# Strided attention: four groups per store in the place of their Q blocks, dense turned weights, values 512 columns wide

## The chip, the cores and the metric

The kernel runs on one core of one Trainium2 chip. The metric is the device time of one execution in microseconds (us), the median of several runs. A profile is taken of one execution; its span runs from the first to the last instruction, and the execution's own time is a little longer than the span.

A core has five instruction queues that matter here, each in order: PE (matrix products; PEld is its weight loading), DVE, ACT and POOL (elementwise work on 128 partitions), and SP, which here only issues DMA transfers. Semaphores hold a queue's next instruction until another queue or a transfer is done. All transfers of this kernel go through SP's one DMA queue, spread over 16 DMA engines.

## The reference

Batch 8 and 12 heads make 96 heads, each with 1024 queries of 64 numbers (float32). Every query attends to the same 16 keys of its head, those at positions 0, 64, 128 and so on:

```python
q = Q[:, :, i:i + 1, :]
k = K[:, :, attend_positions, :]       # 16 keys
v = V[:, :, attend_positions, :]
scores  = einsum('bhqd,bhkd->bhqk', q, k) * scale
weights = exp(scores - max(scores))
weights = weights / (sum(weights) + 1e-10)
result  = einsum('bhqk,bhkd->bhqd', weights, v)
```

Q is 25.2 MB and so is the result. Of K and V only 0.4 MB each is needed. Arithmetic is small beside the 51 MB that have to be moved.

## The kernel before

**Tiling.** The 96 heads are cut into 24 groups of four heads (`HG = 4`, `NG = 24`). One group is 1 MiB of Q, 8 KB in each of 128 partitions, and 1 MiB of result.

**The way of one group g**, with the engine of each step:

- `load(g)` (SP): 1 MiB of Q into one of 11 blocks `qn` (`QBUFS = 11`).
- `cast(g)` (POOL, L307; for groups 0 to 2 shared with ACT, L302 and L304): to bf16 in `qb`.
- `transpose(g)` (DVE, L319): `qb` in 32x32 blocks of 4-byte words to `qt`.
- `scores(g)` (PE, L327): 16 products of 64 columns with the keys `k_t` into `sc`.
- `largest(g)` (DVE, L341 and L344): row maximum, and subtraction into the single buffer `low`.
- `raise_(g)` (ACT, L349): exponential into `ex`.
- `sums(g)` (DVE, L354 and L357): sum and reciprocal `rec`.
- `weights(g)` (POOL, L364): `ex * rec` to bf16 `wt`.
- `turn(g)` (PE, L371): four transposes of `wt` into `tp`.
- `spread(g)` (ACT, L383): two instructions copy `tp` to `wb`, each scaled by one column of the 0/1 mask `sel`, so that `wb` holds eight tiles of 128x128, half of each zero.
- `outputs(g, n)` (PE, L391), n = 0 and 1: four products of 256 columns each with the values `v_all`, into one half of the four-bank tile `o`.
- `evict(g, n)` (ACT, L411): that half of `o` to the block `out_sb` of the group. There are 8 such blocks (`OBUFS = 8`).
- `store(g, n)` (SP): single groups for the first 14 (`SINGLE = 14`) and for group 22, pairs between; the last group goes out by itself at the end. One row of result written in memory is 4 KB (16 queries of a head).

**The order of the work** is written out by hand. One turn i of the loop records the steps of several groups, newest first; the digit is how many groups a step lags behind (`cast-1` is group i + 1, `evA4` is group i - 4):

```python
ORDER = "transpose0 cast-1 values2 turn3 spread3 sums2 outA4 largest1 evA4 outB4 evB4 scores0 weights2 raise_1 queue4".split()
```

Each engine takes its own steps in that order. On POOL, therefore, `cast(i + 1)` stands ahead of `weights(i - 2)`; on DVE `transpose(i)`, `values`, `sums(i - 2)`, `largest(i - 1)`; on ACT `spread(i - 3)`, two evictions of group i - 4, `raise_(i - 1)`. `queue(i - 4)` puts a group's store and then the next loads on SP, so a load stands behind a store that waits for its evictions.

**Keys and values.** K and V are loaded once. `keys` (ACT, L278) places the keys in `k_t`. `values` (POOL, L291) copies the values from `v_raw` into `v_all`, which POOL had cleared (L264): 16 copies of 32 partitions in the turns 2 to 6, behind the casts.

**Waits.** `Program` records every step with what it reads and writes and turns that into semaphore waits; PE runs in a hardware loop and waits on counters (`gate`) instead. A step that carries a gate signals nothing else: who waits for `evict(g, 1)`, as a store does, waits for the next ACT step behind it, `raise_`.

Of the kernel before, what the change touches and what calls it, by code (L numbers as in the profile page):

```python
# [168 lines left out]
def kernel(  # L169
# [8 lines left out]
    nc = tc.nc  # L178
# [12 lines left out]
    QBUFS = 11  # L191
    OBUFS = 8
    RUN = 2
    SINGLE = 14
# [5 lines left out]
    qn = [sb.tile([P, 32 * D], FP32, name=f"qn{i}") for i in range(QBUFS)]  # L200
    out_all = [sb.tile([P, RUN, 2, 16, D], FP32, name=f"out_sb{i}") for i in range(OBUFS // RUN)]
    out_sb = [out_all[i // RUN][:, i % RUN] for i in range(OBUFS)]
    late = out_all[-1].rearrange("p n b x d -> p (n b x d)")
    k_raw = late[:, 0 : NC * D].rearrange("p (n d) -> p n d", d=D)
    k_half = late[:, NC * D : 2 * NC * D].bitcast(BF16).rearrange("p (a n d) -> p a n d", a=2, d=D)
    k_bf, k_r = [k_half[:, i] for i in range(2)]
# [6 lines left out]
    v_all = sb.tile([P, NG + 4, 4, D], BF16, name="v_all")  # L213
# [26 lines left out]
    def load_rows(name, tile_, src, lane):  # L240
        op("SP", lambda: nc.sync.dma_start(tile_, _ap_with(src, kv_src)),
           writes=[name], lane=lane)

    load_rows("k_raw", k_raw, K, f"out{OBUFS - 2}")
    load(0)
    load_rows("v_raw", v_raw, V, f"out{OBUFS - 1}")
    for g in range(1, QBUFS):
        load(g)
# [10 lines left out]
       writes=[f"wb{i}{a}" for i in range(2) for a in range(2)])  # L259
# [4 lines left out]
    op("POOL", lambda: nc.gpsimd.memset(v_all, 0.0),  # L264
       writes=[f"v{c}{a}{b}{m}" for c in range(2) for a in range(2) for b in range(2) for m in range(2)] + ["none"])
# [19 lines left out]
    parts = (slice(0, 2), slice(2, NC))  # L285
# [3 lines left out]
    def values(c, a, b, m):  # L289
        src, dst, part = 32 * (2 * c + b), 32 * (2 * a + b), parts[m]  # L290
        op("POOL", lambda: nc.gpsimd.tensor_copy(  # L291
            out=v_all[dst : dst + 32, 3 + c + 2 * part.start : 3 + c + 2 * part.stop - 1 : 2, 2 * a + b],
            in_=v_raw[src : src + 32, part],
        ), reads=["v_raw"] + apart, writes=[f"v{c}{a}{b}{m}"])
        apart[:] = [f"v{c}{a}{b}{m}"]
# [3 lines left out]
    def cast(g, shared):  # L299
        q, b = qn[g % QBUFS], qb[g % 2]  # L300
        if shared:
            op("ACT", lambda: nc.scalar.copy(b[:, half:], q[:, half:]),  # L302
               reads=[f"qn{g % QBUFS}1"], writes=[f"qb{g % 2}1"])
            op("POOL", lambda: nc.gpsimd.tensor_copy(out=b[:, 0:half], in_=q[:, 0:half]),  # L304
               reads=[f"qn{g % QBUFS}0"], writes=[f"qb{g % 2}0"])
        else:
            op("POOL", lambda: nc.gpsimd.tensor_copy(out=b, in_=q),  # L307
               reads=[f"qn{g % QBUFS}{h}" for h in range(2)] + apart,
               writes=[f"qb{g % 2}{h}" for h in range(2)])
            apart[:] = [f"qb{g % 2}0"]  # L310

    def transpose(g):
        k_in = {0: "0", 1: "1"}.get(g)
        words = qt[g % 2].bitcast(I32)
        if g >= NG:
            op("DVE", lambda: nc.vector.memset(qt[g % 2][:, 0:2], 0.0), reads=["low"], writes=[f"qt{g % 2}"],
               gate="turned")
            return
        op("DVE", lambda: nc.vector.transpose(  # L319
            _ap_with(words, [words.ap[0], [1, 2], [D, 16], [2, 32]]), qb[g % 2].bitcast(I32),  # L320
        ), reads=[f"qb{g % 2}0", f"qb{g % 2}1"] + [f"k_t{k_in}{h}" for h in range(4) if k_in],
           writes=[f"qt{g % 2}"], gate="turned")
# [37 lines left out]
    def weights(g):  # L360
        if g >= NG:
            op("POOL", lambda: nc.gpsimd.memset(wt[g % 2][:, 0:1, 0:2], 0.0), writes=[f"wt{g % 2}"], gate="weighted")
            return
        op("POOL", lambda: nc.gpsimd.tensor_tensor(  # L364
            out=wt[g % 2], in0=ex[g % 2],
            in1=rec[g % 2].unsqueeze(2).to_broadcast([P, 32, NK]), op=ALU.mult,
        ), reads=[f"ex{g % 2}", f"rec{g % 2}"] + [k for k in apart if k[0] == "v"], writes=[f"wt{g % 2}"], gate="weighted")

    def turn_products(g):
        for c in range(4):  # L370
            r = nc.tensor.transpose(  # L371
                tp_ps[g % 2][:, 2 * c : 2 * c + 2].rearrange("p a b -> p (a b)"),
                wt[g % 2][:, 8 * c : 8 * c + 8].rearrange("p t k -> p (t k)"), identity,
            )
        return r
# [5 lines left out]
    def spread(g):  # L381
        for a in range(2):
            op("ACT", lambda a=a: nc.scalar.activation(  # L383
                out=wb[g % 2][:, :, 64 * a : 64 * a + 64], in_=tp_ps[g % 2],
                func=AF.Copy, scale=sel[:, a : a + 1],
            ), reads=[f"tp{g % 2}", "sel"], writes=[f"wb{g % 2}{a}"])

    def output_products(g, k, n):
        for c in range(2 * n, 2 * n + 2):
            for u in range(2):  # L390
                r = nc.tensor.matmul(  # L391
                    _ap_with(
                        o_ps, [o_ps.ap[0], [128, 2], [256, 2], [1, D]],
                        extra_offset=512 * c + D * u,
                    ),
                    lhsT=wb[g % 2][:, 2 * c + u],
                    rhs=v_all[:, k].rearrange("p s d -> p (s d)"), start=True, stop=True,
                )
        return r

    def outputs(g, n):
        op("PE", None, reads=[f"wb{g % 2}0", f"wb{g % 2}1"] + [
               f"v{g % 2}{a}{b}{int(g >= 4)}" if 0 <= g < NG else "none" for a in range(2) for b in range(2)
           ], writes=[f"o{n}"], gates=[(f"free{n}", g + 1)] if g >= 0 else [], looped=True)

    def evict(g, n):
        to = out_sb[g % OBUFS].rearrange("p b (c x) d -> p c b (x d)", c=4)
        half = slice(2 * n, 2 * n + 2)
        plain = g >= NG - 1 - 2 * n
        ready = [f"wb{(g + 1) % 2}0", f"wb{(g + 1) % 2}1"] * (n == 0)  # L410
        op("ACT", lambda: nc.scalar.copy(  # L411
            to[:, half], o_ps[:, half].rearrange("p c (b x) -> p c b x", b=2)
        ), reads=[f"o{n}"] + ready, writes=[f"out{g % OBUFS}.{n}"] + ["k_raw", "k_bf", "k_r"] * (g == OBUFS - RUN and not n),
           after=[stored[g - OBUFS]] if g >= OBUFS and not n else [],
           gate=None if plain else f"free{n}", last=g == NG - 1 and n == 1)

        if plain:
            free([f"out{g % OBUFS}.{n}"], n)
# [12 lines left out]
    def store(g, n):  # L431
        both = range(g, g + n)
        sent = op("SP", lambda: send(g, n), lane=f"out{g % OBUFS}",
                  reads=[f"out{i % OBUFS}.{n}" for i in both for n in range(2)])
        stored.update((i, sent) for i in both)
# [20 lines left out]
    cast(2, True)  # L456
    sums(0)
# [5 lines left out]
    quadrants = [[(c, a, b, m) for c in range(2) for a in range(2) for b in range(2)] for m in range(2)]  # L463
    VALUES = {0: quadrants[0]}
    VALUES.update((i + 1, quadrants[1][2 * i : 2 * i + 2]) for i in range(4))

    DEPTH = 4
    turns = (NG + 4) // TURN
    ahead = 1

    def queue(g):
        for n in range(g + QBUFS + ahead if g else QBUFS, g + QBUFS + ahead + 1):
            if n < NG:
                load(n)
        if g < SINGLE or g == NG - 2:
            store(g, 1)
        elif g % RUN == RUN - 1 and g < NG - 1:
            store(g - RUN + 1, RUN)

    def at(i, stage, lag):  # L480
# [3 lines left out]
        if stage == "transpose" and 0 <= g < NG + 4:  # L484
# [3 lines left out]
        elif stage == "weights" and 0 <= g < NG + 2:  # L488
# [7 lines left out]
        elif stage in ("evA", "evB") and g == -1:  # L496
            n = int(stage == "evB")
            free(["wb00", "wb01"], n)
# [42 lines left out]
    end = send(NG - 1, 1)  # L541
# [34 lines left out]
```

## Time and profile before

| | |
|---|---|
| median of 3 runs | 129.38 us (129.22 to 129.51) |
| the profiled execution's own time | 128.91 us |
| its span | 126.7 us |
| busy PE / DVE / ACT / POOL | 67.0 / 86.4 / 96.8 / 81.8 us |
| DMA: moved, share of 16 engines' span that packets took | 51.16 MB, 96.5% |

The page of the profile has the busy time of each engine, the span in 40 slices, the DMA queues, and groups of instructions by line. A row of groups gives the line, engine, operation, output and input tile, count, busy time and the mean of one in ns, and the idle time of the engine ahead of them with what ended it. A row of the timeline gives start and length in us, engine, line, operation, count, and in brackets the idle time ahead of it. A row of windows gives for each engine its busy time and count in a stretch, then the granted PE clock, the share of the DMA engines' time and GB/s.

### The profile page before, as it was taken

The page shows a single profiled execution, that of the slowest core. Times are in us where ns is not written, and L with a number is a line of the kernel's source. Part 1 is how long each engine was busy: PE and PEld are TensorE (multiplying, and loading weights), DVE is VectorE, ACT ScalarE, POOL GpSimd, SP SyncE. Part 2 cuts the span into 40 slices and gives each one's busy share as a digit, 9 for nine tenths or more (in the row PEclk, how much of TensorE's full clock was granted, in tenths as well). Part 3 has the DMA queues.
Part 4 walks back from the last instruction along what each step waited for, and adds up shares of the span by engine and source line. Part 5 has one row for each costly group of instructions (what it writes and reads, how often), then busy time and mean ns, then how long its engine had stood idle before and what let it go on. Part 6 is the DMA issues. An engine that isn't in the chain of part 4 may idle for free. (4 is left out here: it accounts for less than half of the span.)

```text
span 126.7 us, 2269 instructions
## 1 busy us (share of the span) xinstructions
PE 67.0 (53%) x784; PEld 48.7 (38%) x784; DVE 86.4 (68%) x129; ACT 96.8 (76%) x133; POOL 81.8 (65%) x73
## 2 busy tenths in 40 slices
PE   0003893055862666665885466474666658867000
PEld 0003571044642454443664344253554436635000
DVE  3614989565967789999999999999999955200000
ACT  4289614137977999999999999999999999996000
POOL 5982388999999977778877777887777123300000
PEclk9999999955599968998569999999689985699955
DMA  1997998989979899999999899899899999999980
GB/s 46 406 445 341 486 455 372 496 383 445 476 305 522 339 432 440 411 437 445 398 442 463 372 465 476 346 502 406 380 416 429 432 419 445 424 429 419 406 357 39
DMA packets 7141, 51.16 MB, mean 404 GB/s; under 512 B 3808, under 2 KB 3808, under 8 KB 3808
## 3 DMA queue, kind: packets, MB, share of 16 engines
q1 hardware_dynamic: 7136, 51.12, 96.5%
q14 instruction: 5, 0.04, 0.1%
HBM read 25.95 MB, written 25.17 MB: 403 GB/s over the span
## 5 line engine op out<-in xcount | busy, mean ns | idle before, releaser
L411 ACT COPY out_sb<-o 128x1024 f32<-128x1024 f32 x48 | 46.3, 1015 | 2.1
L307 POOL CAST qb<-qn 128x2048 bf16<-128x2048 f32 x21 | 39.7, 1889 | 0.1
L391 PE MATMUL o<-v_all,wb_all 128*128 x224 | 38.4, 313 | 2.2 <-ACTq L421 0.7
L364 POOL TENSOR_TENSOR wt_all<-ex,rec 128x512 bf16<-128x512 f32 x24 | 25.4, 1057 | 21.3 <-DVE rec L357 20.7
L383 ACT ACTIVATE wb_all<-tp,sel 128x512 bf16<-128x512 bf16 x48 | 30.4, 690 | 6.3 <-PE tp L371 6.2
L319 DVE STREAM_TRANSPOSE qt<-qb 128x1024 int32<-128x1024 int32 x24 | 29.8, 1240 | 6.3 <-ACT qb L302 3.3
L327 PE MATMUL sc<-k_t,qt 128*128 x448 | 23.4, 209 | 18.7 <-DVE qt L319 13.6
L327 PEld LDWEIGHTS sc<-k_t,qt 128*128 128x128 bf16 x448 | 20.1, 109 | 25.1 <-issue 23.3
L371 PE MATMUL tp<-identity,wt_all 128*128 128x128 bf16 x112 | 12.9, 249 | 29.0 <-POOL wt_all L364 28.5
L391 PEld LDWEIGHTS o<-v_all,wb_all 128*128 128x128 bf16 x224 | 22.6, 113 | 10.8 <-ACT out_sb L411 4.9
L354 DVE TENSOR_REDUCE total<-ex 128x32 f32<-128x512 f32 x24 | 16.3, 680 | 9.7 <-ACT ex L349 9.7
L349 ACT ACTIVATE ex<-low 128x512 f32<-128x512 f32 x24 | 15.4, 641 | 6.2 <-DVE low L344 6.2
L371 PEld LDWEIGHTS tp<-identity,wt_all 128*128 128x128 bf16 x112 | 7.5, 108 | 32.0 <-POOL wt_all L364 31.3
L344 DVE TENSOR_TENSOR low<-sc,top 128x512 f32<-128x512 f32 x24 | 16.6, 692 | 0.8
L341 DVE TENSOR_REDUCE top<-sc 128x32 f32<-128x512 f32 x24 | 15.2, 632 | 1.3 <-PE sc L327 1.3
L357 DVE RECIPROCAL rec<-total 128x32 f32<-128x32 f32 x24 | 8.5, 353 | 0.8
L291 POOL CAST v_all<-v_raw 32x128 bf16<-32x128 f32 (+1 forms) x16 | 8.0, 500 | 1.0
L264 POOL MEMSET v_all<- 128x7168 bf16 x1 | 6.1, 6071 | 0.0
L304 POOL CAST qb<-qn 128x1024 bf16<-128x1024 f32 x3 | 3.1, 1040 | 4.2 <-DMA qn<-in_Q_dram 4.2
L278 ACT COPY k_t<-out_sb 32x384 bf16<-32x384 bf16 x8 | 4.1, 508 | 0.7 <-DVE out_sb L269 0.6
L302 ACT CAST qb<-qn 128x1024 bf16<-128x1024 f32 x3 | 3.1, 1040 | 0.0
L268 ACT CAST out_sb<-out_sb 128x768 bf16<-128x768 f32 x1 | 0.8, 831 | 2.7 <-DMA out_sb<-in_K_dram 2.7
(14 smaller groups left out, 6.4 us busy)
## 6 DMA issues: line engine op xcount, KB each, us to landing
qn<-in_Q_dram SPq DMA_DIRECT2D x24, 1024.0 KB, 15.6
out_dram<-out_sb SPq DMA_DIRECT2D x16, 1024.0 KB, 14.4
out_dram<-out_sb SPq DMA_DIRECT2D x4, 2048.0 KB, 13.4
out_sb<-in_K_dram SPq DMA_DIRECT2D x1, 384.0 KB, 4.4
v_raw<-in_V_dram SPq DMA_DIRECT2D x1, 384.0 KB, 7.1
```

The source lines that it names most:

```text
L307: op("POOL", lambda: nc.gpsimd.tensor_copy(out=b, in_=q), reads=[f"qn{g % QBUFS}{h}" for h in range(2)] + apart, writes=[f"qb{g % 2}{h}" f ...
L319: op("DVE", lambda: nc.vector.transpose(_ap_with(words, [words.ap[0], [1, 2], [D, 16], [2, 32]]), qb[g % 2].bitcast(I32),), reads=[f"qb{g ...
L327: r = nc.tensor.matmul(sc_ps[g % 2][:, 64 * i : 64 * i + 64], lhsT=_ap_with(qt[g % 2], [qt[g % 2].ap[0], [2, P]], extra_offset=2 * P * i + f),
L341: op("DVE", lambda: nc.vector.tensor_reduce(out=m, in_=s, op=ALU.max, axis=mybir.AxisListType.X,), reads=[f"sc{g % 2}"], writes=[f"top{g % ...
L344: op("DVE", lambda: nc.vector.tensor_tensor(out=low, in0=s, in1=m.unsqueeze(2).to_broadcast([P, 32, NK]), op=ALU.subtract,), reads=[f"sc{g ...
L349: op("ACT", lambda: nc.scalar.activation(out=ex[g % 2], in_=low, func=AF.Exp, bias=0.0, scale=scale,), reads=["low"], writes=[f"ex{g % 2}"])
L354: op("DVE", lambda: nc.vector.tensor_reduce(out=total[g % 2], in_=ex[g % 2], op=ALU.add, axis=mybir.AxisListType.X,), reads=[f"ex{g % 2}"] ...
L364: op("POOL", lambda: nc.gpsimd.tensor_tensor(out=wt[g % 2], in0=ex[g % 2], in1=rec[g % 2].unsqueeze(2).to_broadcast([P, 32, NK]), op=ALU.mult,
L371: r = nc.tensor.transpose(tp_ps[g % 2][:, 2 * c : 2 * c + 2].rearrange("p a b -> p (a b)"), wt[g % 2][:, 8 * c : 8 * c + 8].rearrange("p t ...
L383: op("ACT", lambda a=a: nc.scalar.activation(out=wb[g % 2][:, :, 64 * a : 64 * a + 64], in_=tp_ps[g % 2], func=AF.Copy, scale=sel[:, a : a ...
L391: r = nc.tensor.matmul(_ap_with(o_ps, [o_ps.ap[0], [128, 2], [256, 2], [1, D]], extra_offset=512 * c + D * u,), lhsT=wb[g % 2][:, 2 * c + ...
L411: op("ACT", lambda: nc.scalar.copy(to[:, half], o_ps[:, half].rearrange("p c (b x) -> p c b x", b=2)), reads=[f"o{n}"] + ready, writes=[f" ...
```

## The change

- **Blocks.** The 11 Q blocks and 8 result blocks become 16 blocks (`BUFS = 16`), four to a tile `quad`. All of the first 16 loads are issued at the start. The result of group g is evicted into the block that its own Q came in.
- **Stores.** Four groups leave in one store of 4 MiB (`RUN = 4`), six stores in all; group 23's eviction ends the last. A row in memory is now 2 KB (8 queries of a head). Loads 16 to 19 stand on SP behind the store of groups 4 to 7 and wait until the store of groups 0 to 3 has landed; loads 20 to 23 likewise one store later.
- **Weights.** `spread` is one ACT copy; `wb` has four dense tiles of 128x128.
- **Values.** The 0/1 mask goes to the values: `masked` (ACT, two instructions) writes two masked bf16 copies `v_mask`, and `values` on DVE, no longer on POOL, copies them into `v_all`, whose rows are twice as long (8 slots of 64): four copies each of 256, 1536 and 1280 elements in 32 partitions, in the turns i = 2, 3 and 4.
- **Products.** `outputs` is two products of 512 columns in each half, in place of four of 256.
- `transpose` writes its words four apart instead of two apart; `evict` writes runs of 64 numbers instead of 256. K and V are loaded by the same kind of copy as Q. The fillers at the end of the PE loop change.

```diff
-    QBUFS = 11
-    OBUFS = 8
-    RUN = 2
-    SINGLE = 14
+    BUFS = 16
+    RUN = 4
...
+    quads = [sb.tile([P, RUN, 32 * D], FP32, name=f"quad{i}") for i in range(BUFS // RUN)]
+    qn = [quads[i // RUN][:, i % RUN] for i in range(BUFS)]
...
+    def masked(a):
+        op("ACT", lambda: nc.scalar.activation(
+            out=v_mask[:, :, a], in_=v_raw, func=AF.Copy, scale=sel[:, a : a + 1],
+        ), reads=["v_raw", "sel"], writes=[f"v_mask{a}"])
+
+    def values(c, m, a, b):
+        src, dst, part = 64 * c + 32 * b, 64 * a + 32 * b, parts[c][m]
+        slot = 4 * a + 2 * b
+        op("DVE", lambda: nc.vector.tensor_copy(
+            out=v_all[dst : dst + 32, 3 + c + 2 * part.start : 3 + c + 2 * part.stop - 1 : 2, slot : slot + 2],
+            in_=v_mask[src : src + 32, part],
+        ), reads=["v_mask0", "v_mask1"], writes=[f"v{c}{m}{a}{b}"])
...
     def spread(g):
-        for a in range(2):
-            op("ACT", lambda a=a: nc.scalar.activation(
-                out=wb[g % 2][:, :, 64 * a : 64 * a + 64], in_=tp_ps[g % 2],
-                func=AF.Copy, scale=sel[:, a : a + 1],
-            ), reads=[f"tp{g % 2}", "sel"], writes=[f"wb{g % 2}{a}"])
+        op("ACT", lambda: nc.scalar.copy(wb[g % 2], tp_ps[g % 2]), reads=[f"tp{g % 2}"], writes=[f"wb{g % 2}"])
...
         for c in range(2 * n, 2 * n + 2):
-            for u in range(2):
-                r = nc.tensor.matmul(
...
+            r = nc.tensor.matmul(
+                o_ps[:, c], lhsT=wb[g % 2][:, c],
+                rhs=v_all[:, k].rearrange("p s d -> p (s d)"), start=True, stop=True,
+            )
...
     def evict(g, n):
-        to = out_sb[g % OBUFS].rearrange("p b (c x) d -> p c b (x d)", c=4)
+        to = qn[g % BUFS].rearrange("p (h x d) -> p x h d", h=HG, d=D)[:, 4 * n : 4 * n + 4]
...
-    def send(g, n):
-        o = out_sb[g % OBUFS]
+    def send(g):
+        o = quads[g % BUFS // RUN]
         return _copy(
             nc,
-            _ap_with(out, [[16 * D, P], [2 * SD, 2 * n], [1, 16 * D]], g * HG * SD),
-            _ap_with(o, [o.ap[0], [1, 1], [1, 32 * n * D]]),
+            _ap_with(out, [[8 * D, P], [SD, HG * RUN], [1, 8 * D]], g * HG * SD),
+            _ap_with(o, [o.ap[0], [1, 1], [1, 32 * RUN * D]]),
         )
...
     def queue(g):
-        for n in range(g + QBUFS + ahead if g else QBUFS, g + QBUFS + ahead + 1):
-            if n < NG:
+        if g % RUN < RUN - 1 or g == NG - 1:
+            return
+        turn_ = g // RUN
+        store(g - RUN + 1)
+        if 1 <= turn_ <= NG // RUN - BUFS // RUN:
+            first = BUFS + (turn_ - 1) * RUN
+            for n in range(first, first + RUN):
                 load(n)
-        if g < SINGLE or g == NG - 2:
-            store(g, 1)
-        elif g % RUN == RUN - 1 and g < NG - 1:
-            store(g - RUN + 1, RUN)
...
-    end = send(NG - 1, 1)
+    end = send(NG - RUN)
```

More of the change, by code (lines that the diff above doesn't have):

```diff
@@ L199 @@
     edge = sb.tile([P, 32], FP32, name="edge")
[L200 to L206, printed above, removed]
+    quads = [sb.tile([P, RUN, 32 * D], FP32, name=f"quad{i}") for i in range(BUFS // RUN)]
+    qn = [quads[i // RUN][:, i % RUN] for i in range(BUFS)]
+    k_raw = sb.tile([P, NC, D], FP32, name="k_raw")
+    k_bf, k_r = [sb.tile([P, NC, D], BF16, name=f"k_half{i}") for i in range(2)]
     v_raw = sb.tile([P, NC, D], FP32, name="v_raw")
@@ L258 @@
     op("DVE", lambda: nc.vector.memset(wb_all, 0.0),
-       writes=[f"wb{i}{a}" for i in range(2) for a in range(2)])
+       writes=[f"wb{i}" for i in range(2)])
     op("DVE", lambda: nc.vector.tensor_reduce(
@@ L263 @@
     ), reads=["identity"], writes=["sel"])
-    op("POOL", lambda: nc.gpsimd.memset(v_all, 0.0),
-       writes=[f"v{c}{a}{b}{m}" for c in range(2) for a in range(2) for b in range(2) for m in range(2)] + ["none"])
+    op("POOL", lambda: nc.gpsimd.memset(v_all.rearrange("p g s d -> p (g s d)").bitcast(FP32), 0.0),
+       writes=[f"v{c}{m}{a}{b}" for c in range(2) for m in range(2 - c) for a in range(2) for b in range(2)] + ["none"])
     def key_rows():
@@ L283, in keys @@
         ), reads=["k_r"], writes=[f"k_t{c}{h}"])
-    parts = (slice(0, 2), slice(2, NC))
+    parts = ((slice(0, 2), slice(2, NC)), (slice(0, NC),))
     apart = []
[L289 to L295, printed above, removed]
+    def masked(a):
[9 more added lines that the diff above has]
+        ), reads=["v_mask0", "v_mask1"], writes=[f"v{c}{m}{a}{b}"])
     half = 16 * D
     def cast(g, shared):
-        q, b = qn[g % QBUFS], qb[g % 2]
+        q, b = qn[g % BUFS], qb[g % 2]
         if shared:
             op("ACT", lambda: nc.scalar.copy(b[:, half:], q[:, half:]),
-               reads=[f"qn{g % QBUFS}1"], writes=[f"qb{g % 2}1"])
+               reads=[f"qn{g % BUFS}1"], writes=[f"qb{g % 2}1"])
             op("POOL", lambda: nc.gpsimd.tensor_copy(out=b[:, 0:half], in_=q[:, 0:half]),
-               reads=[f"qn{g % QBUFS}0"], writes=[f"qb{g % 2}0"])
+               reads=[f"qn{g % BUFS}0"], writes=[f"qb{g % 2}0"])
         else:
             op("POOL", lambda: nc.gpsimd.tensor_copy(out=b, in_=q),
-               reads=[f"qn{g % QBUFS}{h}" for h in range(2)] + apart,
+               reads=[f"qn{g % BUFS}{h}" for h in range(2)] + apart,
                writes=[f"qb{g % 2}{h}" for h in range(2)])
@@ L366, in weights @@
             in1=rec[g % 2].unsqueeze(2).to_broadcast([P, 32, NK]), op=ALU.mult,
-        ), reads=[f"ex{g % 2}", f"rec{g % 2}"] + [k for k in apart if k[0] == "v"], writes=[f"wt{g % 2}"], gate="weighted")
+        ), reads=[f"ex{g % 2}", f"rec{g % 2}"], writes=[f"wt{g % 2}"], gate="weighted", times=1 if g < NG - 1 else 3)
     def turn_products(g):
@@ L408, in evict @@
         half = slice(2 * n, 2 * n + 2)
         plain = g >= NG - 1 - 2 * n
-        ready = [f"wb{(g + 1) % 2}0", f"wb{(g + 1) % 2}1"] * (n == 0)
+        ready = [f"wb{(g + 1) % 2}"] * (n == 0)
         op("ACT", lambda: nc.scalar.copy(
-            to[:, half], o_ps[:, half].rearrange("p c (b x) -> p c b x", b=2)
-        ), reads=[f"o{n}"] + ready, writes=[f"out{g % OBUFS}.{n}"] + ["k_raw", "k_bf", "k_r"] * (g == OBUFS - RUN and not n),
-           after=[stored[g - OBUFS]] if g >= OBUFS and not n else [],
+            to, o_ps[:, half].rearrange("p c (x h d) -> p (c x) h d", x=2, h=HG)
+        ), reads=[f"o{n}"] + ready, writes=[f"qn{g % BUFS}{n}"],
@@ L431, in store @@
[L431 to L435, printed above, removed]
+            _ap_with(out, [[8 * D, P], [SD, HG * RUN], [1, 8 * D]], g * HG * SD),
+            _ap_with(o, [o.ap[0], [1, 1], [1, 32 * RUN * D]]),
+        )
+    def store(g):
+        op("SP", lambda: send(g), lane=f"out{g % BUFS // RUN}",
+           reads=[f"qn{i % BUFS}{h}" for i in range(g, g + RUN) for h in range(2)])
@@ L456 @@
     cast(2, True)
+    for a in range(2):
+        masked(a)
     sums(0)
@@ L483, in at @@
             return
-        if stage == "transpose" and 0 <= g < NG + 4:
+        if stage == "transpose" and 0 <= g < NG + 2:
             transpose(g)
@@ L487, in at @@
             scores(g)
-        elif stage == "weights" and 0 <= g < NG + 2:
+        elif stage == "weights" and 0 <= g < NG:
             weights(g)
```

56 lines of the change are left out of this document (22 added, 34 removed).

## The prediction

> **What bounds the kernel now.** First the page: the span, the busy times, the DMA line of the 40 slices and the DMA queue.
>
> ```profile
> span 126.7 us, 2269 instructions
> PE 67.0 (53%) x784; PEld 48.7 (38%) x784; DVE 86.4 (68%) x129; ACT 96.8 (76%) x133; POOL 81.8 (65%) x73
> DMA  1997998989979899999999899899899999999980
> q1 hardware_dynamic: 7136, 51.12, 96.5%
> ```
>
> The 16 DMA engines work 0.965 x 126.7 = 122.3 us and stop only at the two ends. The work cannot shrink: the bytes stay. Second, the windows: what a load and a store cost there (last two columns: share of the DMA engines, GB/s).
>
> ```profile
> core 0: us, PE busy (x) PEld busy (x) DVE busy (x) ACT busy (x) POOL busy (x), PEclk, DMA share, GB/s
> 0.00:5.00 5.00, 0.00 (x0) 0.00 (x0) 2.86 (x3) 1.28 (x1) 3.57 (x7) 1.00 0.61 182
> 12.00:34.00 22.00, 13.02 (x147) 10.14 (x145) 16.65 (x24) 10.80 (x16) 18.47 (x23) 0.79 1.00 429
> 100.00:118.00 18.00, 12.36 (x142) 8.76 (x140) 5.78 (x14) 15.53 (x21) 3.31 (x5) 0.81 1.00 423
> ```
>
> Busy 0.61 of 5 us, DMA starts at 2.0. From 12 to 34 it only loads (the first store, issued at 31.15 below, stands behind loads), at 429 GB/s: 1.049 MB take 2.44 us, 24 loads 58.6. From 100 to 118 it only stores (loads land at most 25.4 after their issue, and SP issues none after 74), at 423: 4.19 MB take 9.92, all stores 59.5. K and V get the rest, 122.3 - 58.6 - 59.5 = 4.2. The ends (126.7 - 2.0 - 122.3) are 2.4.
>
> Third, the timelines of ACT and SP, and the waits of SP: how close the computing runs behind.
>
> ```profile
> 18.58 0.63 ACT L349 ACTIVATE ex<-low 128x512 f32<-128x512 f32 x1 [2.95 <-DVE low L344]
> ...
> 42.23 1.93 ACT L411 COPY out_sb<-o 128x1024 f32<-128x1024 f32 x2
> ...
> 44.57 1.27 ACT L383 ACTIVATE wb_all<-tp,sel 128x512 bf16<-128x512 bf16 x2
> 45.92 1.93 ACT L411 COPY out_sb<-o 128x1024 f32<-128x1024 f32 x2
> 47.73 0.64 ACT L349 ACTIVATE ex<-low 128x512 f32<-128x512 f32 x1
> ...
> 112.01 4.17 ACT L411 COPY out_sb<-o 128x1024 f32<-128x1024 f32 x4
> ```
>
> ```profile
> 0.96 0.43 SPq L241 DMA_DIRECT2D out_sb<-in_K_dram  x1
> 1.45 0.74 SPq L34 DMA_DIRECT2D qn<-in_Q_dram  x1
> ...
> 31.15 0.63 SPq L34 DMA_DIRECT2D out_dram<-out_sb  x1
> ...
> 48.40 0.59 SPq L34 DMA_DIRECT2D out_dram<-out_sb  x1
> ...
> 74.24 43.69 SPq L34 DMA_DIRECT2D out_dram<-out_sb  x9
> SPq L571 <- DMA out_dram<-out_sb: 8.0, 1, 8.0
> ```
>
> ```profile
> DMA to landing us min/median/max: 6.6/15.6/25.4
> ```
>
> ACT evicts group 3 at 42.23, group 4 at 45.92: a period of 3.69, without idle time to the end. Computing ends at 116.2, the last 1 MiB store is issued near 117.4 (74.24 + 43.69 is its end) and lands 8.0 later, behind older stores. So DMA is the bound, with ACT 3.69 against DMA's 2.44 + 2.48 = 4.92 per group: the slack lets the stores queue up and no gap open. Load 0, issued at 1.45, lands at the least in 6.6 (row of the Q transfers), at 8.05; DMA had served K (2.1) and it (2.44) by 6.5, so landing is seen 1.5 after service. From issue to service (0.96 to 2.0) is 1.05.
>
> **The change: engines.** Rows of DVE, POOL, PE and four groups:
>
> ```profile
> 16.06 1.19 DVE L319 STREAM_TRANSPOSE qt<-qb 128x1024 int32<-128x1024 int32 x1
> ...
> 23.91 1.25 DVE L319 STREAM_TRANSPOSE qt<-qb 128x1024 int32<-128x1024 int32 x1 [1.28 <-POOL qb L307]
> 25.07 0.64 DVE L354 TENSOR_REDUCE total<-ex 128x32 f32<-128x512 f32 x1
> 25.75 0.35 DVE L357 RECIPROCAL rec<-total 128x32 f32<-128x32 f32 x1
> 26.02 0.63 DVE L341 TENSOR_REDUCE top<-sc 128x32 f32<-128x512 f32 x1
> 26.68 0.69 DVE L344 TENSOR_TENSOR low<-sc,top 128x512 f32<-128x512 f32 x1
> ```
>
> ```profile
> 35.73 1.89 POOL L307 CAST qb<-qn 128x2048 bf16<-128x2048 f32 x1
> 37.68 1.50 POOL L291 CAST v_all<-v_raw 32x640 bf16<-32x640 f32 x2
> 39.33 1.06 POOL L364 TENSOR_TENSOR wt_all<-ex,rec 128x512 bf16<-128x512 f32 x1
> ```
>
> ```profile
> 35.84 0.40 PE L371 MATMUL tp<-identity,wt_all 128*128 128x128 bf16 x4 [1.42 <-POOL wt_all L364]
> 36.08 1.04 PE L391 MATMUL o<-v_all,wb_all 128*128 x8
> ```
>
> ```profile
> L264 POOL MEMSET v_all<- 128x7168 bf16 x1 | 6.1, 6071 | 0.0
> L278 ACT COPY k_t<-out_sb 32x384 bf16<-32x384 bf16 x8 | 4.1, 508 | 0.7 <-DVE out_sb L269 0.6
> L255 DVE MEMSET k_t<- 128x1792 uint32 x1 | 1.6, 1552 | 1.9 <-issue 1.9
> L268 ACT CAST out_sb<-out_sb 128x768 bf16<-128x768 f32 x1 | 0.8, 831 | 2.7 <-DMA out_sb<-in_K_dram 2.7
> L269 DVE STREAM_TRANSPOSE out_sb<-out_sb 128x384 int32<-128x384 int32 x1 | 0.6, 578 | 1.0 <-ACT out_sb L268 1.0
> ```
>
> ACT loses one spread of two, 0.64 per group, and falls to about 3.05. Start to start, DVE needs 1.16 + 0.68 + 0.27 + 0.66 + 0.65 = 3.42 (the last is 0.69 less what it overlaps the next): it becomes the pace of computing. Its words written four apart I price at nothing, since a transposed word costs (1240 - 578)/640 = 1.03 ns whether alone or two apart. `masked` (two of 0.83, as L268) fits ACT's idle 2.95 ahead of 18.58; without it raise_(1) would be late. The clearing of `v_all` has as many elements, now of 4 bytes: 0.85 ns each against 0.87 for DVE's 4-byte memset, so 6.07 again. Four products of 512 columns cost what eight of 256 did, 1.04. Runs of 64 in the eviction are free: L278 writes runs of 16, and (831 - 508)/384 = 0.84 ns an element plus 185 fits both rows and, within 30, the eviction's 1015. POOL sheds 1.5 per turn while `values` lasted (37.68).
>
> New on DVE are twelve copies of 12288 elements together, T. The trace has no DVE copy. From below: a 4-byte write (two bf16) costs 0.87, so 0.43 each, plus 0.06 an instruction, T = 6; from above 1.03 an element, T = 14. Below 6 only if they are hidden, and DVE is the pace. The nearest row is the transposing of 4-byte words, 0.52 per bf16: T = 7. [...]
>
> **The change: DMA, in its one order.** A store's row halves from 4 to 2 KB. A load (8 KB pieces) runs at 9.77 per 4.19 MB, a store (4 KB) at 9.92: 0.15 for 32 more rows per DMA engine, so 64 more cost 0.30: 10.2. From above, K and V pay 4.2 us for 192 rows per engine, 21.9 ns, of which 256 bytes at 429/16 GB/s are 9.5; 64 rows at 12.4 make 10.7. From below, 9.77. I take 10.2.
>
> - K, V and loads 0 to 15 are issued at once: 2.0 + 4.2 + 39.0 = 45.2.
> - DVE: `transpose(2)` ends at 16.06 + 1.16 = 17.2. To the reciprocal of group 2 stand 2 x (1.31 + 1.16 + 0.95) + T, so 24.0 + T = 31.0; group g + 2 follows at 31.0 + 3.42 g. From one group's reciprocal, weights 1.1, turn 0.4, spread 0.65, half the products 0.5, evictions 1.93 make 4.6, which is 1.2 behind the next group's: evict(3) ends at 42.5, evict(7) at 56.1. A store goes 0.55 later (48.40 against 47.85), DMA 1.05 after it.
> - Store 0-3: ready at 44.1, served 45.2 to 55.4. Store 4-7: ready at 57.7. **First gap, 2.3.** Served to 67.9. Before, queued loads filled this; now loads 16 to 19 stand behind that very store: to 77.7. Store 8-11 to 87.9. Load 20 to 90.3, seen at 91.8.
> - POOL takes `cast(20)` ahead of `weights(17)`, so until 91.8 it holds weights(17), and with that turn(17), spread(17), evictions 16 and all later ones. Then 1.89 + 1.06 + 0.4 + 0.65 + 0.5 + 1.93 = 6.4: evict(16) ends at 98.2. Seven more groups at 3.1, between POOL's 2.95 and DVE's 3.42: evict(19) 107.5, evict(23) 119.9. (`cast(16)` does the same at 71.8; evict(15) ends near 88, in time for 97.7.)
> - Loads to 97.7, store 12-15 to 107.9, store 16-19 ready at 109.1 (**gap 1.2**), to 119.3.
> - Last store: issued 1.2 after the last eviction, as now (117.4 against 116.2), plus 1.05: 122.15 (**gap 2.85**), 10.2 long, four groups instead of one, to 132.35. An end of 1.5 (2.4, less what the engines drift apart in an unbroken run): span 133.85, against 126.7. The profiled execution stands 2.2 over its span, the median 2.7; with 2.45, 136.3 us.
>
> **The rivals.**
>
> *No gap opens.* Were evictions always early, 2.0 + 4.2 + 58.6 + 6 x 10.2 + 2.4 = 128.4, or 130.85 us. For it: evict(3) is just in time, and gaps of 1 to 3 hang on sums of many short terms. Against it: POOL's order. 11%.
>
> *Larger packets win.* Each partition now sends 32 KB at once as a load's row does; if stores ran like loads, 9.77, without gaps, the span is 2.0 + 4.2 + 58.6 + 58.6 + 2.4 = 125.8, 128.25 us: faster. It decides as soon as rows cost nothing and all gaps close. Against it, 1 and 2 MiB stores run alike:
>
> ```profile
> 74.00:92.00 18.00, 10.68 (x138) 7.40 (x136) 16.75 (x26) 17.62 (x25) 14.02 (x11) 0.94 0.99 421
> ```
>
> Here, loads and 1 MiB stores mixed, 421; above, mostly 2 MiB, 423. 7%; between it and the last case, no change: 3%. [...]
>
> *Copies one element at a time.* T = 14 moves evict(7) and all behind it by 7: 143.3. For it: every DVE row here costs 1 ns an element. 12%.
>
> *Rows cost as K's do*, or writes 256 KB apart are slow in memory: 10.7 on the four stores of the chain, 2.0: 138.3. 7%.
>
> **How the numbers follow.** The forecast has 60%. Its own terms (T 6 to 9, period 2.95 to 3.42, store 9.9 to 10.7, not all at one end) give 133 to 140. The range goes down to the first rival and up to most of the third: 130.5 to 142.5 leaves out 7 + 3 and half of 12. A run of this kernel can tell 0.2% from no change: faster 7%, same 3%, slower 90%.
>
> **What would show it.** Right: DMA slices under 9 near 56 us, 108 and 120; POOL's longest wait on a Q load ahead of its casts of groups 16 and 20; DVE nearly without idle time from 20 to 65; the span ending some 12 us after the last eviction, with nothing but one 4 MiB store; a DMA share near 92%. Each by itself: ACT near 81 us busy; L391 with half the instructions at twice their length; `values` on DVE near 7 us together; store windows near 411 GB/s. Wrong: a DMA share of 96% or more, or store 16-19 issued before store 12-15 is served.

## The result, and the profile after

The changed kernel takes 149.52 us (median of 4 runs, 149.38 to 150.08) against 129.30 us (129.07 to 129.51) for the kernel before, measured along with it: a ratio of 1.157, 95% interval 1.154 to 1.161. The forecast was 136.3 us with a range to 142.5: the sign held, the size did not.

First the page, with the chain of work that ended last.

```profile
span 147.7 us, 1998 instructions
PE 75.5 (51%) x672; PEld 42.5 (29%) x672; DVE 108.5 (73%) x139; ACT 83.9 (57%) x111; POOL 73.9 (50%) x55
...
DMA  2999999999990299606997999999999916995993
...
q1 hardware_dynamic: 5120, 51.12, 84.6%
...
DVE 59%; DMA 17%; ACT 7%; PE 3%; issue 2%; POOL 2%; SPq 0%; ACTq 0%; DVEq 0%; POOLq 0%
...
L320 DVE STREAM_TRANSPOSE qt<-qb 128x1024 int32<-128x1024 int32 x24 | 48.9, 2037 | 10.0 <-POOL qb L309 6.7
...
L309 POOL CAST qb<-quad 128x2048 bf16<-128x2048 f32 x21 | 39.7, 1892 | 11.5 <-DMA quad<-in_Q_dram 11.3
```

The DMA queue works 0.846 x 147.7 = 125.0 us; before it was 122.3 of 126.7. So of the 21.0 us by which the span grew, 2.7 are more DMA work and 18.3 are DMA standing idle (22.7 against 4.4). The slices show four holes. DVE carries 59% of the chain, and one row on it stands out: a transpose takes 2037 ns where it took 1.2 us before. POOL's casts wait 11.3 us for loads.

The windows of the four holes (columns as before):

```profile
45.00:52.00 7.00, 4.75 (x36) 2.51 (x37) 6.93 (x8) 5.26 (x8) 5.18 (x4) 0.70 0.18 75
62.00:68.00 6.00, 5.21 (x32) 2.55 (x32) 5.93 (x7) 4.68 (x7) 4.58 (x3) 0.50 0.01 5
120.00:124.00 4.00, 2.69 (x40) 1.71 (x40) 3.21 (x8) 2.97 (x5) 1.17 (x2) 1.00 0.10 41
134.00:136.00 2.00, 0.25 (x2) 0.00 (x0) 0.00 (x0) 0.00 (x0) 0.00 (x0) 1.00 0.27 115
```

In the first two, DVE is busy for 6.93 of 7 and 5.93 of 6 us while DMA moves next to nothing: computing has become the bound, and DVE is its pace. (PE's granted clock is low there too, 0.50 in the second hole. But DVE has almost no idle time in it, so it is not PE that DVE waits for.) The timelines say what the holes wait for. SP first:

```profile
50.36 16.98 SPq L34 DMA_DIRECT2D out_dram<-quad  x2
67.38 6.58 SPq L34 DMA_DIRECT2D quad<-in_Q_dram  x4
83.13 0.59 SPq L34 DMA_DIRECT2D out_dram<-quad  x1
83.76 9.51 SPq L34 DMA_DIRECT2D quad<-in_Q_dram  x4
101.40 33.89 SPq L34 DMA_DIRECT2D out_dram<-quad  x3
```

Store 0-3 goes out at 50.36 (forecast 43.05), store 4-7 just ahead of the loads of 67.38 (56.7), the last one at 101.40 + 33.89 = 135.3. Loads 16 to 19 and 20 to 23 stand behind stores that wait. POOL shows who is held by them:

```profile
82.35 1.89 POOL L309 CAST qb<-quad 128x2048 bf16<-128x2048 f32 x1 [4.10 <-DMA quad<-in_Q_dram]
...
103.67 1.89 POOL L309 CAST qb<-quad 128x2048 bf16<-128x2048 f32 x1 [7.17 <-DMA quad<-in_Q_dram]
105.52 1.06 POOL L362 TENSOR_TENSOR wt_all<-ex,rec 128x512 bf16<-128x512 f32 x1
```

`cast(16)` and `cast(20)` wait for their loads, and `weights(17)` starts only when `cast(20)` is over, with no wait of its own. One period of DVE, and ACT's evictions of groups 3, 7, 16 and, in the last row, 22 and 23:

```profile
45.50 2.04 DVE L320 STREAM_TRANSPOSE qt<-qb 128x1024 int32<-128x1024 int32 x1
47.39 0.63 DVE L355 TENSOR_REDUCE total<-ex 128x32 f32<-128x512 f32 x1
48.05 0.35 DVE L358 RECIPROCAL rec<-total 128x32 f32<-128x32 f32 x1
48.32 0.63 DVE L342 TENSOR_REDUCE top<-sc 128x32 f32<-128x512 f32 x1
48.98 0.69 DVE L345 TENSOR_TENSOR low<-sc,top 128x512 f32<-128x512 f32 x1
49.59 2.05 DVE L320 STREAM_TRANSPOSE qt<-qb 128x1024 int32<-128x1024 int32 x1
```

```profile
47.00 1.93 ACT L400 COPY quad<-o 128x1024 f32<-128x1024 f32 x2 [0.27 <-PE o L384]
49.70 0.63 ACT L350 ACTIVATE ex<-low 128x512 f32<-128x512 f32 x1 [0.77 <-DVE low L345]
...
63.41 1.93 ACT L400 COPY quad<-o 128x1024 f32<-128x1024 f32 x2 [0.27 <-PE o L384]
...
108.14 1.93 ACT L400 COPY quad<-o 128x1024 f32<-128x1024 f32 x2 [0.27 <-PE o L384]
...
129.35 4.19 ACT L400 COPY quad<-o 128x1024 f32<-128x1024 f32 x4
```

A turn now takes 49.59 - 45.50 = 4.09 us, where 3.42 was forecast. From the transpose's start to the next instruction's it is now 47.39 - 45.50 = 1.89, where 1.16 was taken; that is the whole of it. The four other instructions cost what they did.

### The profile page after: what moved, and what is told of

Same layout as the page of the kernel before. It is cut to its first block, busy times and chain, and to the rows that moved or that the text cites. A ratio compares the mean times of both kernels' runs of the same rounds, so it can differ in the third digit from the quotient of the medians.

```text
span 147.7 us, 1998 instructions
## 1 busy us (share of the span) xinstructions
PE 75.5 (51%) x672; PEld 42.5 (29%) x672; DVE 108.5 (73%) x139; ACT 83.9 (57%) x111; POOL 73.9 (50%) x55
## 3 DMA queue, kind: packets, MB, share of 16 engines
q1 hardware_dynamic: 5120, 51.12, 84.6%
## 4 chain that ended last, share of the span: by engine, by line
DVE 59%; DMA 17%; ACT 7%; PE 3%; issue 2%; POOL 2%; SPq 0%; ACTq 0%; DVEq 0%; POOLq 0%
DVE qt L320 27%; DMA quad<-in_Q_dram 13%; DVE low L345 8%; DVE top L342 7%; DVE total L355 7%; DVE v_all L294 5%; DVE rec L358 4%; ACT quad L400 3%; DMA k_raw<-in_K_dram 3%; PE o L384 1%; ACT k_t L275 1%; POOL qb L309 1%; PE sc L328 1%; ACT ex L350 1%; POOL wt_all L362 1%
## 5 line engine op out<-in xcount | busy, mean ns | idle before, releaser
L320 DVE STREAM_TRANSPOSE qt<-qb 128x1024 int32<-128x1024 int32 x24 | 48.9, 2037 | 10.0 <-POOL qb L309 6.7
L400 ACT COPY quad<-o 128x1024 f32<-128x1024 f32 x48 | 46.3, 1015 | 4.4 <-PE o L384 3.1
L309 POOL CAST qb<-quad 128x2048 bf16<-128x2048 f32 x21 | 39.7, 1892 | 11.5 <-DMA quad<-in_Q_dram 11.3
L384 PE MATMUL o<-v_all,wb_all 128*128 x112 | 42.5, 517 | 0.6 <-ACTq L409 0.6
L328 PE MATMUL sc<-k_t,qt 128*128 x448 | 26.9, 224 | 25.0 <-DVE qt L320 24.4
L380 ACT COPY wb_all<-tp 128x512 bf16<-128x512 bf16 x24 | 13.8, 577 | 8.9 <-PE tp L369 8.8
L384 PEld LDWEIGHTS o<-v_all,wb_all 128*128 128x128 bf16 x112 | 12.8, 127 | 12.7 <-issue 6.6
L294 DVE COPY v_all<-v_mask 32x256 bf16<-32x256 bf16 (+2 forms) x12 | 7.7, 642 | 0.2
L261 POOL MEMSET v_all<- 128x7168 f32 x1 | 6.1, 6073 | 0.0
L275 ACT COPY k_t<-k_half 32x384 bf16<-32x384 bf16 x8 | 4.1, 508 | 0.7 <-DVE k_half L266 0.6
```

The costliest lines, as they stand in the source:

```text
L294: op("DVE", lambda: nc.vector.tensor_copy(out=v_all[dst : dst + 32, 3 + c + 2 * part.start : 3 + c + 2 * part.stop - 1 : 2, slot : slot + ...
L309: op("POOL", lambda: nc.gpsimd.tensor_copy(out=b, in_=q), reads=[f"qn{g % BUFS}{h}" for h in range(2)] + apart, writes=[f"qb{g % 2}{h}" fo ...
L320: op("DVE", lambda: nc.vector.transpose(_ap_with(words, [words.ap[0], [1, 4], [P, 8], [4, 32]]), qb[g % 2].bitcast(I32),), reads=[f"qb{g % ...
L328: r = nc.tensor.matmul(sc_ps[g % 2][:, 64 * i : 64 * i + 64], lhsT=_ap_with(qt[g % 2], [qt[g % 2].ap[0], [2, P]], extra_offset=2 * P * i + f),
L384: r = nc.tensor.matmul(o_ps[:, c], lhsT=wb[g % 2][:, c], rhs=v_all[:, k].rearrange("p s d -> p (s d)"), start=True, stop=True,)
L400: op("ACT", lambda: nc.scalar.copy(to, o_ps[:, half].rearrange("p c (x h d) -> p (c x) h d", x=2, h=HG)), reads=[f"o{n}"] + ready, writes= ...
```

## The experiments

Two theories for the missing 13 us. *Step*: the transpose is slow because its words are written four apart, and DVE at 4.1 us a group makes every 4 MiB store late. *Stores*: the big stores, their place ahead of the loads and their shorter rows cost more than forecast, and the slow transpose is hidden as it would have been under the old kernel's slack.

**Words two apart in the changed kernel**, nothing else.

```diff
-    [1, 4], [P, 8], [4, 32]
+    [1, 2], [D, 16], [2, 32]
```

> The changed kernel, with the transpose writing its words two apart as before; rows of the result then hold other queries. Step theory (the four-word step makes a transpose 2.04 us long, DVE the pace at 4.10 per group, and everything behind it late): transposes back to 1.24, DVE at 3.4 per group, evict(3) ready before the loads end at 45, last eviction near 121.5 in place of 133.5, span near 134.5, time near 136.5 us. Store theory (six stores of four groups, 2 KB rows and loads behind stores set the time whatever DVE does): above 146 us.

Measured: 140.35 us, ratio to before 1.085 (1.083 to 1.088). The span and the transposes on its page:

```profile
span 137.9 us, 1998 instructions
...
L320 DVE STREAM_TRANSPOSE qt<-qb 128x1024 int32<-128x1024 int32 x24 | 29.6, 1235 | 15.1 <-POOL qb L309 11.8
```

Both theories lose their pure form. The step takes 9.2 us of the 20.2, and 802 ns of every transpose; 11 us are left without it, and 4 of them the forecast did not have.

**The same step in the kernel before**, the other way round: words four apart, nothing else.

```diff
-    [1, 2], [D, 16], [2, 32]
+    [1, 4], [P, 8], [4, 32]
```

> The kernel before, with only the transpose's write step changed to four words; rows hold other queries. Step theory: 2.04 each, DVE 4.1 per group against ACT's 3.69, the last eviction at 122 to 124 in place of 116.2. DMA keeps single-group stores and queued loads, so few gaps: only the last 1 MiB stores come late, span 129.5 to 131, time 132 to 133.5 us. So the same slow transposes cost the kernel before 3 us where they cost the changed one 13. Store theory: no change of the transposes, or none of the time, 129.3.

Measured: 132.07 us, ratio 1.020 (1.017 to 1.023). On its page the same duration:

```profile
L319 DVE STREAM_TRANSPOSE qt<-qb 128x1024 int32<-128x1024 int32 x24 | 48.9, 2039 | 4.3 <-ACT qb L302 3.3
```

So the duration belongs to the step and not to the kernel around it. But the same 19 us of DVE cost the old kernel 2.7 (132.07 against 129.42 beside it) and the new one 9.2. Two things differ there: the old kernel has no 4 MiB stores, and its ACT already takes 3.69 us a group, which hides most of DVE's 4.10. This pair doesn't part them; the square further down changes only the stores, with the loads behind them.

**How far apart is too far?** The old kernel with a different step for each group (1, 2, 4, 8, 16, 32 words, in the order of its lines L322 to L327).

```diff
+    step = (1, 2, 4, 8, 16, 32)[g % 6]
+    to = _ap_with(words, [words.ap[0], [1, step] if step > 1 else [32, 1], [32 * step, 32 // step], [step, 32]])
```

> The kernel before, with the transpose's write step taken in turn from 1, 2, 4, 8, 16 and 32 words, four groups each, on lines of their own; rows hold other queries. If the cost follows the distance in bytes: 1.24 at one and two words, 2.04 at four, and more than that at eight and beyond. If four words is a threshold alone: 2.04 from four on. If it hangs on the order of the blocks and not on the step: no clear row.

Its groups, by line:

```profile
L324 DVE STREAM_TRANSPOSE qt<-qb 128x1024 int32<-128x1024 int32 x4 | 8.2, 2061 | 0.0
L325 DVE STREAM_TRANSPOSE qt<-qb 128x1024 int32<-128x1024 int32 x4 | 8.2, 2045 | 0.0
...
L323 DVE STREAM_TRANSPOSE qt<-qb 128x1024 int32<-128x1024 int32 x4 | 5.0, 1238 | 0.0
L322 DVE STREAM_TRANSPOSE qt<-qb 128x1024 int32<-128x1024 int32 x4 | 4.9, 1237 | 3.3 <-ACT qb L302 3.3
```

One and two words apart cost the same, four and eight both 0.8 us more; 16 and 32 (1930 and 1966 ns) are no worse. It is not a slope but a step, between two and four.

**Where in between, and is it the distance?** The old kernel with ten Q blocks and 18 extra transposes of 256 words into a tile that nobody reads: one, two, three and four words apart, each block of 32 in a field of its own, four interleaved (as the change does it), and two in fields 128 words apart.

```diff
+        lambda: nc.vector.transpose(words_to([[32, 8], [1, 32]]), qb[0][:, 0:512].bitcast(I32)),
+        lambda: nc.vector.transpose(words_to([[64, 8], [2, 32]]), qb[0][:, 0:512].bitcast(I32)),
+        lambda: nc.vector.transpose(words_to([[96, 8], [3, 32]]), qb[0][:, 0:512].bitcast(I32)),
+        lambda: nc.vector.transpose(words_to([[128, 8], [4, 32]]), qb[0][:, 0:512].bitcast(I32)),
+        lambda: nc.vector.transpose(words_to([[1, 4], [128, 2], [4, 32]]), qb[0][:, 0:512].bitcast(I32)),
+        lambda: nc.vector.transpose(words_to([[128, 8], [2, 32]]), qb[0][:, 0:512].bitcast(I32)),
```

> The kernel before with 10 Q blocks and, early on, 18 more transposes of 256 words into a tile that nothing reads, each form three times on a line of its own: words 1, 2, 3 or 4 apart with each block of 32 in a field of its own, words 4 apart with four blocks laid into one another as the changed kernel does, and words 2 apart in fields 128 apart. Only the length of these instructions is asked for. Distance theory (a step of 16 bytes or more halves the rate of the write): about 0.43 us for 1, 2 and 3 words, 0.65 for both forms of 4, 0.43 for 2 words in wide fields. Interleaving theory (blocks written into one another collide): 0.65 only where four blocks share a field. Field theory (blocks 128 words apart): 0.65 for the last form too.

One tile's instructions, by line (shortest/median/longest in ns):

```profile
L455 DVE STREAM_TRANSPOSE apart_words<-qb x3: 403/445/445, 11.2 to 17.8; 128x256 int32<-128x256 int32 x3
L456 DVE STREAM_TRANSPOSE apart_words<-qb x3: 446/446/446, 11.6 to 18.3; 128x256 int32<-128x256 int32 x3
L457 DVE STREAM_TRANSPOSE apart_words<-qb x3: 516/517/539, 12.1 to 18.7; 128x256 int32<-128x256 int32 x3
L458 DVE STREAM_TRANSPOSE apart_words<-qb x3: 628/629/631, 12.6 to 19.3; 128x256 int32<-128x256 int32 x3
L459 DVE STREAM_TRANSPOSE apart_words<-qb x3: 627/628/635, 13.3 to 20.0; 128x256 int32<-128x256 int32 x3
L460 DVE STREAM_TRANSPOSE apart_words<-qb x3: 446/447/448, 14.0 to 20.6; 128x256 int32<-128x256 int32 x3
```

Only the distance between one written word and the next counts: 445 and 446 at one and two, 517 at three, 629 at four. How wide the fields are (447) and whether they interleave (628) does nothing. At three words apart the price lies between; the expectation had put three at 0.43 us. Why the engine pays is not shown here; the distance at which it does is.

**Single stores.** The other suspect: the changed kernel with each group stored by itself, still 2 KB rows, and load g + 12 behind store g.

```diff
+    AHEAD = 4
...
-            _ap_with(out, [[8 * D, P], [SD, HG * RUN], [1, 8 * D]], g * HG * SD),
+            _ap_with(out, [[8 * D, P], [SD, HG], [1, 8 * D]], g * HG * SD),
...
-        if g % RUN < RUN - 1 or g == NG - 1:
+        if g == NG - 1:
             return
...
+        store(g)
+        if AHEAD <= g < NG - BUFS + AHEAD:
+            load(BUFS + g - AHEAD)
```

> The changed kernel, with its slow transposes and its 2 KB rows, but each group stored by itself as soon as it is evicted, and load g + 12 behind the store of group g. Stall theory (the gaps come from stores that wait for the slowest of four groups with loads behind them, and from the 4 MiB at the end): no wait of a cast on a load, DVE at 4.10 without idle time to the end, last eviction near 128, span near 133, time near 135 us. If the 2 KB rows are what costs, DMA stays the bound and the time stays above 140.

Measured: 135.00 us, ratio 1.043 (1.040 to 1.046); POOL's casts by shape:

```profile
L310 POOL CAST qb<-quad 128x2048 bf16<-128x2048 f32 x21 | 39.7, 1890 | 0.2 <-DVE v_all L295 0.2
```

With a load behind each small store no cast waits for a load. DVE now only paces the end: its last eviction ends at 126.9, and the rest of the stores follows.

**Both together**, single stores and words two apart.

> The changed kernel with both causes taken away: words two apart (rows of the result then hold other queries) and each group stored by itself, load g + 12 behind the store of group g. 2 KB rows, dense weights and values 512 columns wide stay. Both theories together say that no gap opens and DMA is the bound again: its work is 125.0 us in the changed kernel's profile (84.6% of 147.7) against 122.3 before, so span 2.0 + 125.0 + 2.4 = 129.4 and time near 131.9 us, 2% over before. If ACT's relief were worth anything by itself: below 129.4. If something else of the change costs time: above 134.

Measured: 130.40 us, ratio 1.009 (1.007 to 1.011). Its page:

```profile
span 127.8 us, 2022 instructions
PE 62.1 (49%) x672; PEld 36.1 (28%) x672; DVE 92.4 (72%) x139; ACT 83.8 (66%) x111; POOL 73.8 (58%) x55
...
DMA  1999989999899989999989989999999999999992
...
q1 hardware_dynamic: 7712, 51.12, 96.8%
```

The holes are gone: DMA works 0.968 x 127.8 = 123.7 us and idles 4.1. That is less than expected (125.0 us of DMA work, 131.9 us). With this run the square is full (medians, us):

| words | stores of 4 MiB | single stores | cost of the stores |
|---|---|---|---|
| four apart | 149.52 | 135.00 | 14.5 |
| two apart | 140.35 | 130.40 | 10.0 |
| cost of the step | 9.2 | 4.6 | |

Two causes, and they feed each other: 10.0 + 4.6 = 14.6 taken one by one, 19.1 together. The kernel before took 129.30, 129.42 and 129.27 us beside these runs, so one or two tenths of such a difference mean nothing. What is left with both taken away, 1.1 us over the kernel before, is about the additional DMA work (123.7 against 122.3); no run takes it apart. ACT, relieved from 96.8 to 83.8 us busy, gains nothing: this version has all the savings of dense weights and is still not faster than before, since DMA is its bound.

**Rows of 2 KB** alone, in the kernel before.

```diff
-            _ap_with(out, [[16 * D, P], [2 * SD, 2 * n], [1, 16 * D]], g * HG * SD),
+            _ap_with(out, [[8 * D, P], [SD, HG * n], [1, 8 * D]], g * HG * SD),
```

> The kernel before, with its stores written in 2 KB rows of four heads in place of 4 KB rows of two (the rows hold other queries); nothing else. Row theory: DMA's work grows by the 2.7 us by which the changed kernel's DMA time exceeds that of before, and DMA is the bound: 131.5 to 132.5 us. If the additional DMA time of the changed kernel came from its 4 MiB stores or from its gaps and not from the rows: 129.4.

Measured: 129.38 us, ratio 1.001 (0.999 to 1.003). Its page:

```profile
span 127.2 us, 2269 instructions
...
q1 hardware_dynamic: 7136, 51.12, 96.8%
```

DMA works 0.968 x 127.2 = 123.1 us, 0.8 more than before for all 25 MB, in one profile of each, and the time doesn't show it. The theory that short rows cost 2.7 us falls: row length is out as a cause.

**Loads ahead of the stores.** Stores of 4 MiB and words four apart stay; on SP the four loads that follow a store's turn go ahead of it.

```diff
-        store(g - RUN + 1)
         if 1 <= turn_ <= NG // RUN - BUFS // RUN:
             ...
                 load(n)
+        store(g - RUN + 1)
```

> The changed kernel, with loads 16 to 19 (and 20 to 23) ahead of the store of groups 4 to 7 (8 to 11) on SP instead of behind it, so that they wait for the landing of the older store alone. Stall theory: they fill the gap of DMA from 62 to 68, load 16 is there when its cast comes, load 20 some 6 us earlier than its 103.6, the last eviction and the end 4 to 6 us earlier: 144 to 146 us. If the pace of DVE alone set the end, no more than 1 us: 148.5.

Measured: 143.50 us, ratio 1.110 (1.107 to 1.112), a little under what was expected. Two lines of its page, and SP's timeline:

```profile
DMA  1999999999998039947998993999899999999993
...
L309 POOL CAST qb<-quad 128x2048 bf16<-128x2048 f32 x21 | 39.7, 1891 | 0.4 <-DMA quad<-in_Q_dram 0.4
```

```profile
51.40 0.61 SPq L34 DMA_DIRECT2D out_dram<-quad  x1
63.68 2.40 SPq L34 DMA_DIRECT2D quad<-in_Q_dram  x4
...
87.69 2.41 SPq L34 DMA_DIRECT2D quad<-in_Q_dram  x4
```

The casts hardly wait for loads any more (0.4 us, 11.3 in the changed kernel). So the order on SP is worth 6.0 of the 14.5 us that the big stores cost. The holes left (a slice is 3.56 us) end with what SP then issues: store 0-3 at 51.40, and the two sets of loads at 63.68 and 87.69. From 89 us on there is none.

**The copies of the values, undisturbed.** The first four copies of `values` meet two casts on POOL. Here `cast(3)` is held till they are done.

```diff
-               reads=[f"qn{g % BUFS}{h}" for h in range(2)] + apart,
+               reads=[f"qn{g % BUFS}{h}" for h in range(2)] + apart + [f"v00{a}{b}" for a in range(2) for b in range(2)] * (g == 3),
...
-    ORDER = "transpose0 cast-1 values2 turn3 spread3 sums2 outA4 largest1 evA4 outB4 evB4 scores0 weights2 raise_1 queue4".split()
+    ORDER = "transpose0 values2 cast-1 turn3 spread3 sums2 outA4 largest1 evA4 outB4 evB4 scores0 weights2 raise_1 queue4".split()
```

> The changed kernel, with cast(3) on POOL held until the first four copies of the values on DVE are done. Exclusion theory (a copy of this kind and a POOL instruction do not run together, so that the 256-element copies, 894 ns in the mean and 1832 the longest, waited for casts): all four near 220 ns, 0.9 together in place of 3.63, and with evict(7) and the first gap 2 to 3 us earlier, 147 to 148 us. If the small copies are slow by themselves: still near 894 each, and the time 149.5 or later.

Measured: 147.53 us, ratio 1.141 (1.138 to 1.144). The copies of the changed kernel, by shape, and then the first four of them on DVE's timeline in both kernels, the changed one first:

```profile
L294 DVE COPY v_all<-v_mask 32x256 bf16<-32x256 bf16 x4 | 3.6, 894 | 0.1
L294 DVE COPY v_all<-v_mask 32x1536 bf16<-32x1536 bf16 x4 | 2.2, 552 | 0.1
L294 DVE COPY v_all<-v_mask 32x1280 bf16<-32x1280 bf16 x4 | 1.9, 482 | 0.0
```

```profile
19.65 3.63 DVE L294 COPY v_all<-v_mask 32x256 bf16<-32x256 bf16 x4
```

```profile
19.52 0.89 DVE L294 COPY v_all<-v_mask 32x256 bf16<-32x256 bf16 x4
```

A copy of 256 elements takes longer than one of 1536 while POOL casts: 894 ns against 552. In the changed kernel the four took 1307, 217, 1832 and 219 ns, and each of the two long ones ended 0.07 us after a cast that had begun before it (20.96 against 20.89, 23.05 against 22.98). With the cast held the four take 0.89 us, so 2.74 of 3.63 were waiting, and the time drops by 2.0. What makes a copy wait for a cast is not shown here.

## Why the prediction was right or wrong

The forecast's steps against the run with words two apart (which has everything it foresaw, without the step) and the changed kernel, in us:

| step | forecast | two apart | changed |
|---|---|---|---|
| one transpose | 1.24 | 1.24 | 2.04 |
| DVE per group | 3.42 | 3.38 | 4.10 |
| `values` on DVE | 7 | 8.8 | 7.7 |
| evict(3) ends | 42.5 | 44.9 | 48.9 |
| store 0-3 issued | 43.1 | 45.8 | 50.4 |
| evict(7) ends | 56.1 | 58.4 | 65.3 |
| `cast(16)` / `cast(20)` start | 71.8 / 91.8 | 75.0 / 96.2 | 82.4 / 103.7 |
| evict(16) ends | 98.2 | 102.6 | 110.1 |
| evict(23) ends | 119.9 | 123.8 | 133.5 |
| span | 133.85 | 137.9 | 147.7 |

- **The step that failed:** "Its words written four apart I price at nothing, since a transposed word costs (1240 - 578)/640 = 1.03 ns whether alone or two apart." The mechanism that follows from it, DVE as the pace and stores that wait for it, was in the sum; the term was mis-sized: 0.80 us a transpose, and 4.10 - 3.38 = 0.72 of each group's turn. The two rows behind it are right (445 and 446 ns in the run of single steps), but neither has four apart, and the text extended them across the place where the price rises. It gave no upper bound for this edit, and so the range had no room for it. Without this one term, with words two apart, the measured 140.35 lies inside the range.
- **Where 0.8 a group became 9.2 us.** Against the run with two apart, evict(3) is 4.0 late and evict(7) 6.9. Then nothing is added for a while: `cast(16)`, `cast(20)` and evict(16) are 7.4 to 7.5 late, since there the loads set the pace. From evict(16) to evict(23) the seven groups take 23.5 instead of 21.2 us, 2.3 more, and the span is 9.8 longer. With single stores DMA's share is still 0.98 from 85 to 100 us, and 0.70 from 110 to 120. Only the end is late there, and 4.6 are left.
- **Copies: 7 forecast, 7.7 and 8.8 measured.** Where POOL did nothing beside them, copies of 1536 and 1280 elements took 552 and 482 ns in the changed kernel; the row of 4-byte words that was taken, 0.52 per bf16, gives 799 and 666. With the first four at 0.89 (the run that holds `cast(3)`) the twelve come to 0.89 + 2.25 + 1.97 = 5.1, and the waiting for casts adds 2.74. So that 7 was near the 7.7 is in part luck: two terms that were left out, the faster copies and the waiting, nearly cancel. No run shows the 9 at which the forecast let T end; the most measured was 8.8, with words two apart.
- **Issue of a store: 0.55 forecast behind its last eviction, 1.4 measured, 0.9 with words two apart.** A store waits for the next `raise_` on ACT. Before, ACT ran without idle time; now `raise_` itself waits 0.77 for DVE's `low` (row at 49.70; 0.26 with words two apart), as DVE is the pace. The forecast had made DVE the pace and kept ACT's old timing for this term.
- **From `cast(16)` to `cast(20)`: 20.0 forecast, 21.3 measured in both kernels.** That is four loads and one store, so these run a little longer than 9.77 + 10.2. Not the rows: they were 0.8 us at the most over the whole kernel. Total DMA work is 123.7 us with single stores of 2 KB rows and 125.0 with six big ones; why is open.
- **Right:** POOL's order. From `cast(20)` to the end of evict(16), 6.4 us were worked out, and 103.67 to 110.07 is 6.4. Also the end: 13.95 forecast from the last eviction to the end of the span, 14.2 measured, one 4 MiB store with nothing beside it. ACT was 83.9 us busy (81 forecast), and L384 had half of the instructions (x112).
- **Signs that missed:** the DMA share, 84.6% where 92% was named (90.6% with words two apart), and the length of the products of 512 columns, 517 ns against 313 before, 1.65 times and not twice.
- **The rivals.** "No gap opens" and "Larger packets win" fall by the holes. "Copies one element at a time" has the time (143.3) that comes nearest, but not the mechanism: the copies took 7.7 us, not 14. (Its own rows give 12288 x 1.03 + 12 x 60 ns = 13.4, and 142.7.) "Rows cost as K's do" falls with 129.38 us for shorter rows.

Put together, from the table's rows: with words two apart evict(3) is 2.4 late, of which the copies are 1.8 and a later start of `transpose(2)` (16.43 against 16.06) 0.4. The issue of the store adds 0.4, the transfers up to `cast(16)` 0.4 and those up to `cast(20)` 1.2. The last seven groups give 0.5 back. The span is 4.0 over the forecast, and so is the time, 140.35 against 136.3. The step adds 9.2: 149.52. That these smaller terms add up is worked out from rows; of them only the waiting of the copies was taken away in a run of its own, in the changed kernel.

## What to carry to other kernels

Before an access pattern is called free, find a row with that very distance: on DVE's transposes here, words two apart cost nothing (1238 against 1237 ns for one) and words four apart 65% more (2037 against 1235). A large store was a gate here: it was ready only with its last part, the loads behind it in its queue waited with it (POOL's casts waited 11.3 us for loads, 0.4 with the loads ahead of the store), and at the end it was one long transfer with nothing beside it (14.2 us from the last eviction to the end of the span); so count a slower engine together with the gates behind it: the same slow transposes cost 4.6 us here with single stores and 9.2 with six large ones. Relieving an engine that has slack (ACT, 13 us less) bought nothing (130.40 against 129.27 us with both causes taken away), and the layout that it called for put its price on the engine next in line.

## What the runs showed of the hardware that was not expected

- A DVE transpose of 4-byte words costs the same with its words one or two apart (1237 and 1238 ns for 1024 words), and at four apart it takes 1.65 times as long (2037 against 1235 ns); from 4 to 32 words the price is flat (1930 to 2061 ns).
- A bf16 copy of 256 elements on DVE took up to 1832 ns beside POOL's casts, 192 ns at the least without them.
- Store rows of 2 KB instead of 4 KB cost no time that could be measured (129.38 against 129.27 us), with 25 MB stored; DMA work in one profile of each is 123.1 against 122.3 us.
